# First MLP, first half: three pairs by seven half-size products instead of two, their input's block sums formed a stage earlier and carried through DRAM

## The chip, the cores and the metric

The kernel runs on one core of a Trainium2 chip. The metric is device microseconds of one execution. Before the change the median of three runs is 1082.24 us (1081.54 to 1082.41).

## The reference

A two-layer decoder trunk on a sequence of 512 tokens with 1024 channels. Layer 0 mixes tokens by a short gated convolution, layer 1 by native sparse attention; each layer ends in a squared-ReLU MLP with 4096 hidden channels:

```python
def short_conv_mixer(h, w_in, conv_w, w_out):
    b_gate, c_gate, u = jnp.split(h @ w_in, 3, axis=-1)
    ...
    return (b_gate * conv) @ w_out

def squared_relu_mlp(h, w1, w2):
    return jnp.square(jax.nn.relu(h @ w1)) @ w2

def reference(x, ...):
    for layer in range(DEPTH):
        h = rms_norm(x, norm_mix[layer])
        if layer < N_A_LAYERS:
            x = x + short_conv_mixer(h, a_w_in[layer], a_conv_w[layer], a_w_out[layer])
        else:
            x = x + nsa_mixer(h, b_w_qg[i], b_w_o[i], shared, rel_bias)
        x = x + squared_relu_mlp(rms_norm(x, norm_mlp[layer]), mlp_w1[layer], mlp_w2[layer])
        ...
    return rms_norm(x, final_norm)
```

The change touches layer 0's `w_out` product and the `h @ w1` of layer 0's MLP.

## The kernel before

**Arithmetic.** Inputs and results are 32 bits wide. For TensorE (PE) every matrix is split into a high and a low 16-bit half (`whi`, `wlo` for weights; `xsh`, `xsl` for activations; `rh`, `rl` for the hidden layer), and each product is three matmuls: high by high, high by low, low by high. So every block of weights that arrives in `wst` is converted: ScalarE (ACT) writes the high half (lines 219 and 239), VectorE (DVE) the low half (lines 220 and 240).

**Tiles.** Activations lie with channels on the 128 partitions and the 512 tokens along the row; `X` is the residual stream, eight such chunks. A product is made for one *pair* at a time, 256 output channels, as two PSUM banks of 128 channels by 512 tokens: `pair` runs over eight chunks of input, 48 matmuls of 512 columns (lines 410 to 412). The MLP is done in two halves of 2048 hidden channels: eight pairs of up-projection (`mlp_up`), then four pairs of down-projection (`mlp_down`), and so again. The first half of layer 0's MLP follows directly on the output projection of the convolution mixer (the loop at lines 627 to 637, four calls of `pair`).

**Seven products.** Some pairs are computed by a recursion of Strassen's kind (`seven`, line 672). Weights and activations are seen as two-by-two blocks (128 channels by 128 channels; 128 channels by 256 tokens), and the four block results come from seven block products instead of eight. A seven runs over four double chunks: 84 matmuls of 256 columns (line 687). It needs

- sums of weight blocks: the weights come into `wst2` as blocks, `block_sums` (lines 153 to 158) adds four more blocks on DVE, and seven blocks instead of four are converted (lines 219, 220);
- sums of activation blocks: `form_sums` (line 462) makes, for each of four double chunks, a scaled copy of `X` on ACT (line 465), three DVE operations of `turned_sums` (lines 168 and 170), and a split into halves (lines 431 and 433). They stay in four places (`places`): the tiles `up_s`, and then `ssacc`, `sq` and two of `rb`, which the mean square uses first;
- copies on ACT of the PSUM banks between products (`keep`, line 698) and DVE additions (lines 713, 716, 720) before the squared ReLU.

`UP_SEVEN` says which pairs (0 to 7) of which half are done so; `mlp_pieces` orders the weights accordingly. In before these are pairs 4 and 6 of the first half.

**Where the sums are formed.** In before `early_sums` forms the four blocks of the first half behind pairs 0 and 1. The first two go to their places; the other two are first put into rows of the hidden layer's tiles `rh` and `rl`, since `ssacc`, `sq` and `rb` still hold the mean square, and `move_sums` brings them over by four transfers on GpSimd's (POOL) queue (line 746).

**Around it.** The mean square's root (`ss.rstd`) is made in pair 1, and its broadcast row `rb` (line 376) late in pair 1; only then can `put_relu` treat pairs 0 and 1 (lines 661 to 670: scale and clip, square, `token_sums` for the down-projection, split). A plain pair's result goes through `put_relu` between products of the seven behind it. `ahead` converts weights ahead of use: two plain pieces, or three blocked ones; blocked weights wait behind the root's last operation (`root_op`).

**Queues.** Weights are loaded on SyncE's (SP) queue. Every engine runs its own instructions in the order in which a list scheduler wrote them down: program order is the priority, and work that the planner expects to be ready may be drawn forward. Tiles of the convolution stage lie in a pool `first`, which is closed behind the output projection; the MLP's pool takes over its memory.

Of the kernel before, what the change touches and what calls it, by code (L numbers as in the profile page):

```python
# [10 lines left out]
F32 = mybir.dt.float32  # L11
F16 = mybir.dt.float16
# [39 lines left out]
def body(ctx, tc, x, rel_bias, norm_mix, norm_mlp, mlp_w1, mlp_w2, a_w_in, a_conv_w, a_w_out,  # L52
         kv_norm, w_kv, cmp_pe_k, cmp_pe_v, phi_k_w1, phi_k_w2, phi_v_w1, phi_v_w2,
         b_w_qg, b_w_o, final_norm, ident_c, onehot_c, out):
    nc = tc.nc
# [6 lines left out]
    dram = ctx.enter_context(pool("dram", space=DRAM))  # L62
# [42 lines left out]
            pieces.append(([v[c + k, :, :, c0:c0 + 256] for k in range(2)], None, scale))  # L105

    BY_SEVEN = ((2, 2), (3, 0), (3, 2))
    UP_SEVEN = (((4, 6), (0, 2, 4, 6)), ((6,), (0, 2, 4, 6)))

    v = a_w_in[0].rearrange("(c p) (s n) -> c p s n", p=128, s=3)  # L110
    for c in range(8):
# [67 lines left out]
    def blocked(i):  # L179
        return pieces[i][1] is None  # L180
# [82 lines left out]
    def ahead():  # L263
        while pos["cv"] < len(pieces) and pos["cv"] < pos["use"] + (AHEAD2[0] if blocked(pos["cv"]) else AHEAD):
            yield from convert_piece()

    def drain(gen):
        for _ in gen:
            pass
# [3 lines left out]
    wk = [first.__enter__()]  # L273
# [30 lines left out]
    xt = [xt4[:, t] for t in range(4)]  # L304
# [155 lines left out]
    sums = []  # L460

    def form_sums(sums, c, gname, z, add_up=token_sums):

        for m in range(2):
            ACT.activation(z[:, 2 * m:2 * m + 2].rearrange("p k n -> p (k n)"), X[:, 2 * c + m], AF.Copy,
                           scale=vec[:, gain[gname] + 2 * c + m:gain[gname] + 2 * c + m + 1])
        add_up(z)
        split_to(sums[c][0], sums[c][1], z[:, 4:8])
# [42 lines left out]
    for p in range(4):  # L511
# [57 lines left out]
        for i, dst in enumerate((pc, pu, pb)):  # L569
# [19 lines left out]
            for m in range(2):  # L589
# [9 lines left out]
                elif dst is pu:  # L599
                    if m == 0:  # L600
                        convs = []
                    v = ftile("cv_v", 2, S + 2)
# [21 lines left out]

    xs = new_split(work, "xs")
    ss = SumSq()
    for p in range(4):
        po = [acc(), acc()]
        pair(ys, po)
        if p < 3:  # L630
            drain(ahead())
        for m in range(2):
            residual_in(po[m], 2 * p + m, 1.0 / (SY * SW))
            ss.add(X[:, 2 * p + m])
        for m in range(2):
            split_gain(xs, 2 * p + m, X[:, 2 * p + m], "mlp0")
        drain(ahead())
    first.__exit__(None, None, None)
    NS2[0], NW2[0], AHEAD2[0] = 3, 4, 3

# [4 lines left out]
    def mlp_up(xs, ss, rh, layer, half, rb, sums):  # L645
        gname = f"mlp{layer}"
# [5 lines left out]
        def new_z():  # L652
            return wk[0].tile([128, 8, 256], F32, name="ml_z", bufs=2)
# [72 lines left out]
        def places():  # L726

            tags = 4 * ((wk[0], "up_s", 4),) + ((work, "ssacc", 1), (work, "sq", 1)) + 2 * ((work, "rb", 3),)
            for i in range(0, 8, 2):
                yield [u.tile([128, 4, 256], F16, name=name, bufs=n) for u, name, n in tags[i:i + 2]]  # L730

        def early_sums(c):

            if c < 2:
                sums.append(next(at))
                form_sums(sums, c, gname, new_z(), turned_sums)
            else:
                staged_sums[c] = [u[:, 4 + c, 0:4] for u in rh]
                form_sums(staged_sums, c, gname, new_z(), turned_sums)

        def move_sums():

            for c in (2, 3):
                sums.append(next(at))
                for u, v in zip(sums[c], staged_sums[c]):
                    nc.gpsimd.dma_start(u, v)

        at, staged_sums = places(), {}
        by_seven = UP_SEVEN[layer][half]
        early = half == 0 and layer == 0 and by_seven  # L750
        behind = range(1, 5) if by_seven else range(4, 8)
# [1 line left out]
        held, post, tag = None, iter(()), ""  # L753
        if half == 0:
            ss.thirds()
        for p in range(8):
            own = half or by_seven and p >= by_seven[0]
            tag = ("c" if tag == "a" else "a") if own else ("bcabcb" if by_seven else "bcabcabc")[p]
            if p in by_seven:
                z = new_z()  # L760
                post = put_relu(p, seven(p, xs, z, post, tag), z)
                continue
            drain(post)
            ph = [bank(tag) for _ in range(2)]
            mid = {1: {1: ss.rstd, 6 if early else 4: root_rows}}.get(p) if half == 0 else None
            pair(xs, ph, mid=mid)
            drain(ahead())
            if early and p < 2:
                for c in (2 * p, 2 * p + 1):
                    early_sums(c)  # L770
            if p == 0 and half == 0:
                held = ph
                continue
            if held:
                drain(put_relu(0, held, new_z()))
                held = None
            post = put_relu(p, ph, new_z())
            if p + 1 not in by_seven:
                drain(post)
            if early and p == 2:  # L780
                move_sums()
            if half == 0 and not early and p in behind:
                sums.append(next(at))
                form_sums(sums, p - behind[0], gname, new_z(), turned_sums)
# [105 lines left out]
    with pool("hidden_a") as hp:  # L890
        wk[0] = hp
        rh = first_half(hp, xs, ss, 0)
# [13 lines left out]
    with pool("attn") as ap:  # L906
# [579 lines left out]
        for i in range(len(items) + 6):  # L1486
# [18 lines left out]
            for part in ("stages", "background") if frees else ("background", "stages"):  # L1505
                if part == "background":
                    while credit > 0.0:
                        u = next(bg, "end")
# [21 lines left out]
    with pool("hidden_b") as hp:  # L1530
        wk[0] = hp
        rh = first_half(hp, xs, ss, 1)
        xsh, xsl = (work.tile([128, 2, D], F32, name=n) for n in ("xsh", "xsl"))
        xt = [(xsh, xsl)[t // 2][:, t % 2] for t in range(4)]
# [163 lines left out]
```

## Time and profile before

| | before |
|---|---|
| median of three runs | 1082.24 us |
| the profiled execution | 1083.04 us |
| its span, first to last instruction | 1080.0 us |
| busy PE / DVE / ACT / POOL | 1067.5 / 958.1 / 621.7 / 75.2 us |
| granted TensorE clock over the span | 0.998 |
| output projection, PE | 132.2 to 173.6 us |
| up-projection, first half of layer 0 | 173.6 to 254.8 us |
| down-projection, first half of layer 0 | 254.8 to 328.2 us |

The profile shows one execution. PE is TensorE's matmuls, PEld its weight loads, DVE VectorE, ACT ScalarE, POOL GpSimd, SP SyncE. Rows of groups read: line, engine, operation, output <- inputs, shapes, count, busy time and mean duration, and idle time of the engine ahead of them with what ended it. Rows of the order of time read: start, duration, engine, line, operation, tiles. Durations of neighbouring operations overlap by some 0.1 us.

### The profile page before, as it was taken

How to read it: one execution, taken by the hardware profiler on the slowest of the kernel's cores; microseconds unless marked ns; L12 is line 12 of the kernel's file. 1: busy time of each engine (PE TensorE's matmuls, PEld its weight loads, DVE VectorE, ACT ScalarE, POOL GpSimd, SP SyncE). 2: the span in 40 equal slices, each digit the busy share in tenths (PEclk: the TensorE clock that was granted, in tenths of full speed). 3: DMA queues.
4: the chain of work that ended last, by engine and by line, in shares of the span. 5: the costliest groups of instructions: out<-in, count | busy, mean ns of one | idle time of the engine just before them, and what ended most of it. 6: DMA issues, size and time to landing. Idle time of an engine off the chain costs nothing.

```text
span 1080.0 us, 21256 instructions
## 1 busy us (share of the span) xinstructions
PE 1067.5 (99%) x8486; PEld 740.5 (69%) x8486; DVE 958.1 (89%) x1688; ACT 621.7 (58%) x974; POOL 75.2 (7%) x113
## 2 busy tenths in 40 slices
PE   9999999999999999999999999999999999999997
PEld 4446644477887758874867677775446788766896
DVE  5898757999998999999478899996999999999996
ACT  5663246565334674548577887874666433566453
POOL 1000000000000000000110104211000000002022
PEclk9999999999999999999999999999999999999999
DMA  8344124333433334312443442201542333333221
GB/s 260 112 147 134 40 81 154 125 99 109 137 101 115 104 113 155 119 44 95 126 139 102 143 138 81 61 21 60 166 127 70 106 111 124 98 101 98 98 99 78
DMA packets 117698, 118.50 MB, mean 110 GB/s; under 512 B 7276, under 2 KB 114496, under 8 KB 117600
## 3 DMA queue, kind: packets, MB, share of 16 engines
q1 hardware_dynamic: 114384, 110.77, 32.6%
q10 hardware_dynamic: 2512, 4.70, 1.3%
q0 software_dynamic: 704, 1.68, 0.5%
q8 instruction: 66, 1.08, 0.4%
q14 instruction: 32, 0.26, 0.1%
HBM read 110.22 MB, written 2.14 MB: 104 GB/s over the span
## 4 chain that ended last, share of the span: by engine, by line
PE 72%; DVE 18%; ACT 3%; issue 3%; DMA 3%; POOL 1%; SPq 0%; ACTq 0%; DVEq 0%; POOLq 0%
PE b L833 6%; PE c L411 5%; PE c L410 5%; PE c L412 4%; PE a L833 4%; PE c L833 4%; PE a L412 4%; PE a L687 4%; PE a L410 4%; PE a L411 4%; DVE wlo L220 4%; PE e L833 3%; PE b L412 3%; PE b L411 3%; PE c L1340 3%
## 5 line engine op out<-in xcount | busy, mean ns | idle before, releaser
L219 ACT ACTIVATE whi<-wst 128x1792 f16<-128x1792 f32 x92 | 153.9, 1692 | 120.9 <-DVE wst L158 72.1
L220 DVE SCALAR_TENSOR_TENSOR wlo<-wst,whi 128x1792 f16<-128x1792 f32 x92 | 185.5, 2022 | 6.5 <-ACT whi L219 6.4
L833 PEld LDWEIGHTS <-whi 128*128 128x128 f16 x1768 | 173.0, 98 | 20.3
L240 DVE SCALAR_TENSOR_TENSOR wlo<-wst,whi 128x1024 f16<-128x1024 f32 (+4 forms) x118 | 129.2, 1101 | 20.6 <-ACT whi L239 20.3
L239 ACT ACTIVATE whi<-wst 128x1024 f16<-128x1024 f32 (+4 forms) x118 | 111.1, 950 | 61.8 <-PE a L411 21.9
L412 PEld LDWEIGHTS <-wlo 128*128 128x128 f16 x800 | 78.1, 98 | 86.5 <-DVE wlo L240 1.0
L410 PEld LDWEIGHTS <-whi 128*128 128x128 f16 x800 | 78.2, 98 | 78.9 <-ACT whi L239 0.6
L411 PEld LDWEIGHTS <-whi 128*128 128x128 f16 x800 | 78.2, 98 | 78.4
L833 PEld LDWEIGHTS <-wlo 128*128 128x128 f16 x884 | 86.5, 98 | 10.9 <-DVE wlo L220 0.2
L669 ACT ACTIVATE rh<-ml_z 128x1792 f16<-128x1792 f32 x32 | 54.1, 1693 | 58.2 <-DVE ml_z L164 58.2
L411 PE MATMUL c<-xsl,whi 128*128 128x512 f16 x224 | 85.0, 379 | 0.0
L412 PE MATMUL c<-xsh,wlo 128*128 128x512 f16 x224 | 85.0, 379 | 0.0
L410 PE MATMUL c<-xsh,whi 128*128 128x512 f16 x224 | 85.0, 379 | 0.0
L1327 ACT ACTIVATE at_p<-at_s,at_m 128x384 f32<-128x384 f32 (+3 forms) x128 | 71.0, 556 | 20.9 <-DVE at_m L1325 20.7
L158 DVE TENSOR_TENSOR wst<-wst 128x256 f32<-128x256 f32 x184 | 78.3, 432 | 2.1
L156 DVE TENSOR_TENSOR wst<-wst 128x512 f32<-128x512 f32 x92 | 63.8, 697 | 15.3 <-DMA wst<-mlp_w_dram 15.1
L833 PE MATMUL b<-rh,whi 128*128 128x256 f16 x256 | 69.2, 273 | 0.0
L833 PE MATMUL b<-rh,wlo 128*128 128x256 f16 x256 | 69.2, 273 | 0.0
L833 PE MATMUL b<-rl,whi 128*128 128x256 f16 x256 | 67.8, 273 | 0.0
L687 PEld LDWEIGHTS <-whi 128*128 128x128 f16 x616 | 60.2, 98 | 7.9
L670 DVE TENSOR_TENSOR rl<-ml_z,rh 128x1792 f16<-128x1792 f32 x32 | 64.7, 2023 | 0.4 <-ACT rh L669 0.4
L1325 DVE CUSTOM_DVE_ANT_0 at_s<-b,T 128x384 f32<-128x384 f32 (+3 forms) x128 | 59.1, 485 | 4.9 <-PE b L1318 4.7
(437 smaller groups left out, 2911.7 us busy)
## 6 DMA issues: line engine op xcount, KB each, us to landing
wst<-mlp_w_dram SPq DMA_DIRECT2D x172, 256.0 KB, 2.9
wst<-mlp_w_dram SPq DMA_DIRECT2D x42, 512.0 KB, 3.7
wst<-a_w_in_dram SPq DMA_DIRECT2D x12, 512.0 KB, 3.5
wst<-w_kv_dram SPq DMA_DIRECT2D x12, 512.0 KB, 3.5
wst<-a_w_out_dram SPq DMA_DIRECT2D x8, 512.0 KB, 3.4
wst<-b_w_qg_dram SPq DMA_DIRECT2D x8, 512.0 KB, 3.6
wst<-b_w_o_dram SPq DMA_DIRECT2D x8, 512.0 KB, 3.6
T<-ext_d ACTq DMA_DIRECT2D x6, 528.0 KB, 3.9
```

The lines of the kernel that those rows point to most:

```text
L158: DVE.tensor_tensor(b[:, :, o], b[:, :, x], b[:, :, y], op=OP.add)
L219: ACT.activation(hi, b[:, :, 1:], AF.Copy, scale=sc)
L220: lows[0] = DVE.scalar_tensor_tensor(lo, b[:, :, 1:], sc, hi, op0=OP.mult, op1=OP.subtract)
L239: ACT.activation(hi[:, s:e], w, AF.Copy, scale=sc)
L240: DVE.scalar_tensor_tensor(lo[:, s:e], w, sc, hi[:, s:e], op0=OP.mult, op1=OP.subtract)
L410: PE.matmul(ps, w[0], xs[0], start=start, stop=False, **k)
L411: PE.matmul(ps, w[0], xs[1], start=False, stop=False, **k)
L412: return PE.matmul(ps, w[1], xs[0], start=False, stop=stop, **k)
L670: DVE.tensor_tensor(rh[1][:, p], z[:, 1:8], rh[0][:, p], op=OP.subtract)
L687: PE.matmul(ps[:, 0:256], l, r, start=first and c == 0 and n == 0, stop=c == 3 and n == 2, skip_group_check=not first)
L833: mm = PE.matmul(acc7[i], wl if n == 1 else wh, xl if n == 2 else xh, stop=c == closes[i] and n == 2, start=c == 0 and n == 0 and not othe ...
L1327: self.weighed = ACT.activation(self.p[:, w], lg[:, w], AF.Exp, bias=mn[:, j:j + 1], scale=-1.0, accum_out=l[:, br * 4 + h:br * 4 + h + 1])
```

## The change

Pairs 3, 5 and 7 of the first half are done in seven products instead of pairs 4 and 6 (counted from 1, as in the change's name: 4, 6 and 8). The block sums of the MLP's input are formed in the output projection, one double chunk behind each of its four pairs, in a tile `told` that lies where the convolution's sums lay. From there each block goes to DRAM (`sums_d`) in two transfers on POOL's queue, and `fetch_sums` reads it back on the same queue: two blocks at the start of the up-projection, two behind pair 1, when their places are free. `early_sums`, `move_sums` and the detour through `rh` and `rl` go.

```diff
--- before.py
+++ after.py
@@ -105,7 +105,7 @@
             pieces.append(([v[c + k, :, :, c0:c0 + 256] for k in range(2)], None, scale))
 
     BY_SEVEN = ((2, 2), (3, 0), (3, 2))
-    UP_SEVEN = (((4, 6), (0, 2, 4, 6)), ((6,), (0, 2, 4, 6)))
+    UP_SEVEN = (((3, 5, 7), (0, 2, 4, 6)), ((6,), (0, 2, 4, 6)))
 
     v = a_w_in[0].rearrange("(c p) (s n) -> c p s n", p=128, s=3)
     for c in range(8):
@@ -624,6 +624,8 @@
 
     xs = new_split(work, "xs")
     ss = SumSq()
+    kept_sums = dram.tile([4, 2, 128, 4, 256], F16, name="sums_d")
+    told = wk[0].tile([128, 2, 4, 4, 256], F16, name="xt")
     for p in range(4):
         po = [acc(), acc()]
         pair(ys, po)
@@ -635,6 +637,10 @@
         for m in range(2):
             split_gain(xs, 2 * p + m, X[:, 2 * p + m], "mlp0")
         drain(ahead())
+        form_sums({p: [told[:, k, p] for k in range(2)]}, p, "mlp0",
+                  wk[0].tile([128, 8, 256], F32, name="xz", bufs=1), turned_sums)
+        for k in range(2):
+            nc.gpsimd.dma_start(kept_sums[p, k], told[:, k, p])
     first.__exit__(None, None, None)
     NS2[0], NW2[0], AHEAD2[0] = 3, 4, 3
 
@@ -729,23 +735,14 @@
             for i in range(0, 8, 2):
                 yield [u.tile([128, 4, 256], F16, name=name, bufs=n) for u, name, n in tags[i:i + 2]]
 
-        def early_sums(c):
-
-            if c < 2:
+        def fetch_sums(n):
+
+            for c in range(len(sums), n):
                 sums.append(next(at))
-                form_sums(sums, c, gname, new_z(), turned_sums)
-            else:
-                staged_sums[c] = [u[:, 4 + c, 0:4] for u in rh]
-                form_sums(staged_sums, c, gname, new_z(), turned_sums)
-
-        def move_sums():
-
-            for c in (2, 3):
-                sums.append(next(at))
-                for u, v in zip(sums[c], staged_sums[c]):
-                    nc.gpsimd.dma_start(u, v)
-
-        at, staged_sums = places(), {}
+                for k in range(2):
+                    nc.gpsimd.dma_start(sums[c][k], kept_sums[c, k])
+
+        at = places()
         by_seven = UP_SEVEN[layer][half]
         early = half == 0 and layer == 0 and by_seven
         behind = range(1, 5) if by_seven else range(4, 8)
@@ -753,6 +750,8 @@
         held, post, tag = None, iter(()), ""
         if half == 0:
             ss.thirds()
+        if early:
+            fetch_sums(2)
         for p in range(8):
             own = half or by_seven and p >= by_seven[0]
             tag = ("c" if tag == "a" else "a") if own else ("bcabcb" if by_seven else "bcabcabc")[p]
@@ -765,9 +764,8 @@
             mid = {1: {1: ss.rstd, 6 if early else 4: root_rows}}.get(p) if half == 0 else None
             pair(xs, ph, mid=mid)
             drain(ahead())
-            if early and p < 2:
-                for c in (2 * p, 2 * p + 1):
-                    early_sums(c)
+            if early and p == 1:
+                fetch_sums(4)
             if p == 0 and half == 0:
                 held = ph
                 continue
@@ -777,8 +775,6 @@
             post = put_relu(p, ph, new_z())
             if p + 1 not in by_seven:
                 drain(post)
-            if early and p == 2:
-                move_sums()
             if half == 0 and not early and p in behind:
                 sums.append(next(at))
                 form_sums(sums, p - behind[0], gname, new_z(), turned_sums)
```

## The prediction

> **What bounds the kernel now.** I read the page first (busy shares, the chain), then the busy time by stage, then TensorE's order of work around the change, then groups of VectorE instructions there.
>
> ```profile
> span 1080.0 us, 21256 instructions
> ...
> PE 1067.5 (99%) x8486; PEld 740.5 (69%) x8486; DVE 958.1 (89%) x1688; ACT 621.7 (58%) x974; POOL 75.2 (7%) x113
> ...
> PE 72%; DVE 18%; ACT 3%; issue 3%; DMA 3%; POOL 1%; SPq 0%; ACTq 0%; DVEq 0%; POOLq 0%
> ```
>
> TensorE (PE) has work 99% of the span and is most of the chain of work; VectorE (DVE) is second in both. A shorter PE stage is worth its whole saving as long as DVE keeps up. The next rows cut the time at the points where PE changes stage: output projection, pairs 1 to 3 of the first half's up-projection, pairs 4 to 8, the down-projection, and the second half's up-projection.
>
> ```profile
> 132.16:173.60 41.44, 41.44 (x194) 18.82 (x192) 25.49 (x36) 15.68 (x22) 0.00 (x0) 1.00 0.28 87
> 173.60:205.40 31.80, 31.80 (x161) 14.83 (x160) 30.94 (x50) 23.85 (x28) 2.17 (x4) 1.00 0.54 172
> 205.40:254.84 49.44, 49.44 (x313) 30.54 (x312) 48.31 (x66) 28.06 (x27) 0.00 (x0) 1.00 0.33 105
> 328.20:406.91 78.71, 78.28 (x530) 51.66 (x528) 73.20 (x105) 47.89 (x50) 0.00 (x0) 1.00 0.36 114
> 254.84:328.20 73.36, 73.36 (x673) 65.75 (x672) 69.59 (x104) 30.55 (x22) 0.00 (x0) 1.00 0.33 109
> ```
>
> Columns: stretch and length, busy PE, weight loads, DVE, ACT, POOL, then clock, DMA share, GB/s. PE is busy without a gap in the first three rows, at full clock. DVE is nearly full in both up rows (30.94 of 31.80, 48.31 of 49.44) and has 16 us to spare in the output projection. So the stage is PE's, with DVE close behind.
>
> **The change, part by part.**
>
> *One more pair as seven products.* Numbering pairs 0 to 7, before has 4 and 6 in seven products, after has 3, 5 and 7. The rows are pairs 4, 5, 6 and 7:
>
> ```profile
> 215.78:224.95 9.17, 9.17 (x85) 8.21 (x84) 9.03 (x18) 6.39 (x9) 0.00 (x0) 1.00 0.32 103
> 224.95:235.31 10.36, 10.36 (x50) 4.70 (x48) 9.46 (x12) 4.92 (x4) 0.00 (x0) 1.00 0.49 152
> 235.31:244.48 9.17, 9.17 (x85) 8.21 (x84) 9.08 (x15) 6.94 (x10) 0.00 (x0) 1.00 0.19 57
> 244.48:254.84 10.36, 10.36 (x50) 4.70 (x48) 10.36 (x10) 5.36 (x4) 0.00 (x0) 1.00 0.47 153
> ```
>
> A seven is 84 weight loads with matmuls 256 columns wide in 9.17 us, a plain pair 48 with 512 columns in 10.36. Three sevens in place of two take **1.19 us** off PE. That is all the gain there is on PE. It lies on the path, since PE waits for nothing here.
>
> *What a seven can cost PE.* It copies PSUM out between products (four ACT copies), and PE can wait for them:
>
> ```profile
> L713 DVE TENSOR_TENSOR ml_z<-b,rh x11: 417/420/423, 221.9 to 981.9; 128x256 f32<-128x256 f32 x11
> 395.25 0.27 PE L687 MATMUL a<-up_s,whi 128*128 128x256 f16 x1 [0.43 <-ACT rl L698]
> ```
>
> There are eleven sevens in the kernel (one L713 in each) and one of them waited 0.43 us. One more is worth 0.04 us; I book 0.05, with 0 and 0.43 as ends.
>
> *Work added and moved on DVE and ACT.*
>
> ```profile
> L168 DVE TENSOR_TENSOR ml_z<-ml_z x4: 684/687/693, 178.3 to 189.1; 128x512 f32<-128x512 f32 x4
> L170 DVE SCALAR_TENSOR_TENSOR ml_z<-ml_z x8: 418/423/425, 179.6 to 193.0; 128x256 f32<-128x256 f32 x8
> L433 DVE TENSOR_TENSOR up_s<-ml_z,up_s x2: 1218/1220/1222, 182.6 to 186.3; 128x1024 f16<-128x1024 f32 x2
> L240 DVE SCALAR_TENSOR_TENSOR wlo<-wst,whi x9: 1196/1221/1226, 174.7 to 242.2; 128x1024 f16<-128x1024 f32 x9
> L156 DVE TENSOR_TENSOR wst<-wst x8: 682/691/699, 189.8 to 254.3; 128x512 f32<-128x512 f32 x8
> L158 DVE TENSOR_TENSOR wst<-wst x14: 415/426/433, 193.3 to 240.6; 128x256 f32<-128x256 f32 x14
> L220 DVE SCALAR_TENSOR_TENSOR wlo<-wst,whi x7: 2019/2022/2029, 201.8 to 252.0; 128x1792 f16<-128x1792 f32 x7
> L661 DVE SCALAR_TENSOR_TENSOR ml_z<-ml_z,rb x4: 417/555/691, 224.7 to 248.6; 128x256 f32<-128x256 f32 x2, 128x512 f32<-128x512 f32 x2
> L664 DVE SCALAR_TENSOR_TENSOR ml_z<-c,rb x4: 680/686/689, 197.0 to 238.5; 128x512 f32<-128x512 f32 x4
> L465 ACT ACTIVATE ml_z<-X,vec 128x512 f32<-128x512 f32 x8 | 5.3, 711 | 2.1 <-DVE up_s L433 2.1
> L431 ACT ACTIVATE up_s<-ml_z 128x1024 f16<-128x1024 f32 x2 | 2.1, 1050 | 0.6 <-DVE ml_z L170 0.6
> ```
>
> (DVE rows: min/median/max in ns, first and last start.) One block of sums takes DVE 0.687 + 2 x 0.423 + 1.220 = 2.75 us, and ACT 2 x 0.711 + 1.050 = 2.47. Four blocks leave pairs 0 and 1: 11.0 us of DVE. Three of them go into the output projection: 8.3 us on 25.49 of 41.44, and 7.4 us on ACT's 15.68. Each engine stays under 82% there, behind a PE that waits for nothing; nothing on the path. Without that room (a block between a residual and its gain) the up-projection's inputs would come up to 2.75 us later. The fourth block needs the last residual and stays behind 173.6.
>
> The third seven brings blocked weights: 0.691 + 2 x 0.426 + 2.022 = 3.57 us a piece for a plain 1.22, so 4.7 us for two pieces. Its own DVE steps are three sums (L713, L716, L720, 0.42 each) and three L661 (0.417 + 0.691 + 0.423) for two L664 (1.37): 1.4 more. Together +6.1 us.
>
> *DVE by stretch.* In the stretch of pairs 0 to 2: 30.94 - 11.0 + 2.75, less two plain conversions for pair 3 (2.4), plus the second blocked piece that pair 3 now needs by its start (3.6; the first stands in the place of pair 4's), plus 2.0 for the low half of pair 1's output, which now fell just behind. That is 25.9 of 31.8, so the first seven is fed in time although it starts 10 us earlier. For pairs 3 to 7 the rest of 79.25 - 11.0 + 2.75 + 6.1 = 77.1 remains: 51.2 us in 49.44 - 1.19 = 48.25. **3.0 us of DVE work spill into the down-projection.** The tightest place there is its second pair's first weights:
>
> ```profile
> 266.89 3.96 DVE L220 SCALAR_TENSOR_TENSOR wlo<-wst,whi 128x1792 f16<-128x1792 f32 x2
> ...
> 273.18 0.27 PE L833 MATMUL d<-rh,whi 128*128 128x256 f16 x1
> ```
>
> The first of the two L220 ends at 268.9 and PE wants it at 273.2: 4.3 us of margin, 1.3 after the spill. So I book no stall, with 0 and 2 us as ends. The down-projection then gives DVE 73.36 - 69.59 = 3.8 us back. The second half's up-projection speaks for this: four sevens in turn with pairs, DVE 73.20 of 78.71, and PE lost 0.43 us in all (78.28 busy).
>
> *The detour through DRAM.* Before, four transfers on POOL's queue move two blocks; after, eight writes and eight reads of 256 KB:
>
> ```profile
> L746 POOL DMA_DIRECT2D ssacc<-rh x1 | 0.6, 560 | 182.3 <-ACT rh L431 182.3
> ...
> L746 POOL DMA_DIRECT2D rb<-rl x1 | 0.5, 536 | 1.0 <-DVE rl L433 1.0
> ...
> out_dram<-xsh SPq DMA_DIRECT2D x2, 512.0 KB, 2.8
> ...
> rb<-rl POOLq DMA_DIRECT2D x1, 256.0 KB, 3.0
> ```
>
> An issue holds POOL's queue 0.54 to 0.56 us, a transfer lands in at most 3.0, and a write of 512 KB to DRAM in 2.8. POOL has no other work here (182.3 us idle before its first). Six writes go during the output projection. Before, the last xsl was done about 178; the fourth block takes 2.75 + 1.05, so it is ready about 182. Then come two writes and eight reads, 10 x 0.56: issued by 188, landed by 191. Pair 3 starts at 205.4 and wants sums in its second product, 1.3 us in. 15 us of cover, so it costs nothing; the bounds are 0 and rival C. A transfer through DRAM of 4.2 MB in all in place of 1 is small beside the 87 and 172 GB/s of these rows. The input tile of the sums and the last block's workspace now live until 182 or 185 in memory that the next pool takes over, so the blocked loads on SP's queue (first wanted at the root's end, about 190) and the plain loads behind them may wait some us; the same 15 us cover them.
>
> The Trainium skill, SBUF — State Buffer, section "A bandwidth-pool intuition that's wrong (but worth ruling out)", speaks against this: a transfer issued from GpSimd takes about 0.62 us alone and 3.1 us against a VectorE copy that locks the shared port. The trace's 0.54 to 0.56 us beside a DVE busy 30.94 of 31.80 do not show it; with 3.1 us for each of ten issues an estimate by that page is 182 + 31 + 3 = 216, some 8 us late, and 1089 us.
>
> **The sum.** The profiled execution took 1083.04 us around its span of 1080.0. 1083.04 - 1.19 + 0.05 = 1081.90. The median of the runs, 1082.24, is 0.80 below that execution; on its footing I predict **1081.1**. About 0.2% (2.2 us) is what can be told from no change, so the whole gain, 0.11%, is half of it.
>
> **The rivals.**
>
> A. *DVE is late* by more than the margin of 1.3 us, at the down-projection's second pair or already at pair 3. For it: DVE's two up rows are full, and the last seven now ends at the stage's end, which no stage of before does. Against: the second half's up-projection. Price 0.5 to 2 us: 1081.6 to 1083.1, the gain eaten.
>
> B. *ACT's queue holds a copy back* (the one that ends on the other side, slower). Place: the first copy of pair 3's seven stands in ACT's queue behind a step that waits for DVE, whose work of pairs 0 and 1 can only start when the row scale is there:
>
> ```profile
> 194.43 0.58 ACT L376 ACTIVATE rb<-e 128x512 f32<-128x512 f32 x1
> ACT rh L669 <- DVE ml_z L164: 13.6, 5, 4.7
> ```
>
> The longest such wait of the stage is 4.7 us. PE has one other product to do meanwhile (9.17 / 7 = 1.3), so the price is up to 3.4 us: 1084.5. It makes the kernel slower once the copy is held over 4.6 us; below that it only eats the gain. Against: 6 us of DVE room ahead of pair 3, which should draw these steps forward.
>
> C. *The sums come late.* If each of the ten issues had to wait for one long DVE operation (2.02 us) they would take 2.6 us each: 182 + 26 + 3 = 211, against the 207.7 at which the last block is wanted: 3.1 us, 1084.2; anything above that is slower than before. Against: the four issue rows. The Trainium skill's rule above would be this rival at its dearest, and the chance of C is the chance I give it.
>
> D. *The change does not do what it says*: the additional seven saves nothing net, because PE's margin is returned later in a wait on DVE or DMA. 1082.2.
>
> E. *More than the sum*: the order of the queues is written anew, and gaps elsewhere close. Over 1 us beyond the 1.19 would have to come from the 12.5 us in which PE is not busy. Below 1080.
>
> **How the numbers follow.** My forecast 0.62 (own range 1080.4 to 1081.7: the span of the runs and the copy's 0.43). A 0.15, D 0.04: both within 0.2%. B 0.07 and C 0.05, taken as slower. E 0.07, faster. So faster 0.07, same 0.62 + 0.15 + 0.04 = 0.81, slower 0.12. The range leaves out E and most of B and C: 1079.9 to 1083.6.
>
> **What would show it.** Right: three stretches of 9.17 us in this up-projection, pairs 3, 5, 7; PE without a gap from 173.6 to the down-projection, which starts about 1.2 us earlier; DVE with idle time around 183 to 193 and late conversions afterwards; POOL issues of about 0.55 us, the last landing before 195. Wrong: a PE wait on ACT's L698 copy in pair 3 (B), on wlo about the down-projection's second pair (A), on a transfer from sums_d (C); or PE gaps in other stages.

## The result, and the profile after

| | before | after |
|---|---|---|
| median | 1081.89 us (1081.45 to 1082.41) | 1094.19 us (1092.42 to 1094.96) |
| span of the profiled execution | 1080.0 us | 1092.0 us |

Four runs each. The ratio is 1.0113, 95% interval 1.0101 to 1.0126: the kernel is 12 us slower, where 1.2 us less had been forecast.

The page after, the lines that answer to those of before:

```profile
span 1092.0 us, 21372 instructions
...
PE 1069.8 (98%) x8522; PEld 745.3 (68%) x8522; DVE 964.2 (88%) x1698; ACT 623.5 (57%) x978; POOL 81.7 (7%) x125
...
PE 71%; DVE 18%; issue 4%; DMA 3%; ACT 3%; POOL 1%; SPq 0%; ACTq 0%; DVEq 0%; POOLq 0%
```

PE's busy time rose by 2.3 us, the span by 12.0, so about 10 us are new idle time. The busy time by stage shows where: output projection; pairs 0 to 2; then pairs 3 to 7, one row each (columns as before).

```profile
132.52:173.96 41.44, 41.44 (x194) 18.80 (x192) 33.30 (x48) 22.25 (x31) 3.28 (x6) 1.00 0.35 108
173.96:206.28 32.32, 31.98 (x162) 14.82 (x161) 18.90 (x32) 12.46 (x15) 5.32 (x10) 1.00 0.61 210
206.28:222.56 16.28, 11.17 (x85) 8.96 (x84) 16.28 (x25) 10.62 (x12) 0.00 (x0) 0.90 0.21 64
222.56:232.92 10.36, 10.36 (x51) 4.70 (x48) 10.36 (x14) 4.34 (x3) 0.00 (x0) 1.00 0.48 153
232.92:244.14 11.22, 9.32 (x85) 8.21 (x84) 8.32 (x14) 7.20 (x9) 0.00 (x0) 1.00 0.16 49
244.14:254.50 10.36, 10.36 (x50) 4.70 (x48) 10.36 (x12) 6.16 (x5) 0.00 (x0) 1.00 0.47 153
254.50:265.23 10.73, 9.33 (x86) 8.21 (x84) 10.73 (x18) 5.43 (x7) 0.00 (x0) 1.00 0.34 113
```

The output projection is 41.44 us as before, with DVE at 33.30 instead of 25.49: three block sums fit there for nothing. But the three sevens take 16.28, 11.22 and 10.73 us instead of 9.17, and DVE, nearly full before, is busy 18.90 of 32.32 us ahead of them. PE's idle time there is these five waits (order of time on PE; brackets: idle time and what ended it):

```profile
206.28 0.27 PE L693 MATMUL c<-xsh,whi 128*128 128x256 f16 x1 [0.34 <-DVE ml_z L670]
...
209.43 0.28 PE L693 MATMUL c<-xsh,wlo 128*128 128x256 f16 x1 [2.23 <-DVE wlo L220]
...
214.34 0.27 PE L693 MATMUL c<-up_s,whi 128*128 128x256 f16 x1 [2.88 <-ACT rh L704]
...
242.84 0.27 PE L693 MATMUL c<-up_s,whi 128*128 128x256 f16 x1 [1.90 <-ACT rl L704]
...
258.68 0.27 PE L693 MATMUL c<-up_s,whi 128*128 128x256 f16 x1 [1.40 <-ACT dn_p L704]
```

The account from 173.96 to 265.23, 91.27 us against 81.24: 80.05 were forecast (81.24 - 1.19), the waits add 8.74, and PE is busy 82.53, that is 2.5 longer, mostly in the first seven, whose granted clock is 0.90. With 0.36 us from the start of the kernel the down-projection begins 10.4 us late. Another 1.36 us are lost in the second half's last seven (11.01 us instead of 9.65; taken up with the last experiments). Together 11.75 of the 12.0 us.

**Why DVE stood.** The queues of POOL and SP after, in order of time (x n: issues grouped in one row):

```profile
183.90 0.54 POOL L643 DMA_DIRECT2D sums_d<-xt  x1 [0.72 <-DVE xt L433]
189.13 2.13 POOL L743 DMA_DIRECT2D up_s<-sums_d  x4 [4.69 <-issue]
...
192.30 1.06 POOL L743 DMA_DIRECT2D rb<-sums_d  x2
```

```profile
188.13 2.93 SPq L192 DMA_DIRECT2D wst<-mlp_w_dram  x6
```

Before, the first blocked loads went out here:

```profile
173.84 1.39 SPq L192 DMA_DIRECT2D wst<-mlp_w_dram  x3
```

The last write of sums is issued at 183.90 and lands at 187.99 us; the first blocked weights of the MLP are asked for 0.14 us behind that, 14.3 us later than before. The reads follow 1.0 us later, so six loads and eight reads of 256 KB each, 3.7 MB, run at once. The stretch from 193 to 198, after:

```profile
193.00:198.00 5.00, 5.00 (x24) 2.25 (x23) 0.19 (x1) 1.70 (x1) 0.37 (x1) 1.00 1.03 379
```

The DMA engines are full (share 1.03, 379 GB/s), and the six loads of 256 KB take 2.65, 2.90, 7.15, 8.87, 11.09 and 11.19 us to land. DVE meanwhile:

```profile
191.57 0.69 DVE L156 TENSOR_TENSOR wst<-wst 128x512 f32<-128x512 f32 x1 [4.21 <-DMA wst<-mlp_w_dram]
192.30 0.89 DVE L158 TENSOR_TENSOR wst<-wst 128x256 f32<-128x256 f32 x2
198.53 0.69 DVE L156 TENSOR_TENSOR wst<-wst 128x512 f32<-128x512 f32 x1 [5.34 <-DMA wst<-mlp_w_dram]
199.25 0.89 DVE L158 TENSOR_TENSOR wst<-wst 128x256 f32<-128x256 f32 x2
201.80 0.69 DVE L156 TENSOR_TENSOR wst<-wst 128x512 f32<-128x512 f32 x1 [1.66 <-DMA wst<-mlp_w_dram]
202.41 2.02 DVE L220 SCALAR_TENSOR_TENSOR wlo<-wst,whi 128x1792 f16<-128x1792 f32 x1
204.35 1.28 DVE L670 SCALAR_TENSOR_TENSOR ml_z<-b,rb 128x512 f32<-128x512 f32 x2
```

DVE stands three times, 11.2 us in all, at the sums of weight blocks. Its queue is in order: the scaling of pair 0 (L670) stands behind them and starts at 204.35. Before, the same step started here:

```profile
195.76 1.29 DVE L664 SCALAR_TENSOR_TENSOR ml_z<-b,rb 128x512 f32<-128x512 f32 x2
```

The row scale that it multiplies by is late as well, since ACT's queue stands on the same sums of blocks: `rb` is made at 201.78 instead of 194.43, behind the conversion of the second piece.

```profile
200.18 1.70 ACT L219 ACTIVATE whi<-wst 128x1792 f16<-128x1792 f32 x1 [5.13 <-DVE wst L158]
201.78 0.58 ACT L376 ACTIVATE rb<-e 128x512 f32<-128x512 f32 x1
```

ACT's squares and splits of pairs 0 and 1 wait for the scaling, and the copies of the seven's PSUM stand behind those in ACT's queue:

```profile
210.74 3.28 ACT L675 ACTIVATE rh<-ml_z 128x1792 f16<-128x1792 f32 x2 [2.83 <-DVE ml_z L164]
213.93 0.36 ACT L704 ACTIVATE rh<-c 128x256 f32<-128x256 f32 x1
```

PE's wait of 2.88 us at 214.34 ends with that copy. This is the theory; its rivals are the extra DMA traffic by itself, the third seven with its DVE work, and the order of DVE's queue.

### The profile page after: what moved, and what is told of

Its sections match the earlier page's. It is cut to its first block, busy times and chain, and to the rows that moved or that the text cites. A ratio compares the mean times of both kernels' runs of the same rounds, so it can differ in the third digit from the quotient of the medians.

```text
span 1092.0 us, 21372 instructions
## 1 busy us (share of the span) xinstructions
PE 1069.8 (98%) x8522; PEld 745.3 (68%) x8522; DVE 964.2 (88%) x1698; ACT 623.5 (57%) x978; POOL 81.7 (7%) x125
## 4 chain that ended last, share of the span: by engine, by line
PE 71%; DVE 18%; issue 4%; DMA 3%; ACT 3%; POOL 1%; SPq 0%; ACTq 0%; DVEq 0%; POOLq 0%
PE b L829 6%; DVE wlo L220 5%; PE c L410 4%; PE c L411 4%; PE c L412 4%; PE a L829 4%; PE c L829 4%; PE a L693 4%; PE a L410 4%; PE a L412 4%; PE a L411 4%; PE e L829 3%; PE c L1336 3%; PE d L829 3%; DMA wst<-mlp_w_dram 3%
## 5 line engine op out<-in xcount | busy, mean ns | idle before, releaser
L219 ACT ACTIVATE whi<-wst 128x1792 f16<-128x1792 f32 x94 | 157.2, 1692 | 130.2 <-DVE wst L158 79.0
L220 DVE SCALAR_TENSOR_TENSOR wlo<-wst,whi 128x1792 f16<-128x1792 f32 x94 | 189.0, 2017 | 6.7 <-ACT whi L219 6.6
L240 DVE SCALAR_TENSOR_TENSOR wlo<-wst,whi 128x1024 f16<-128x1024 f32 (+4 forms) x116 | 126.6, 1098 | 17.4 <-ACT whi L239 17.1
L239 ACT ACTIVATE whi<-wst 128x1024 f16<-128x1024 f32 (+4 forms) x116 | 108.9, 948 | 56.8 <-PE a L411 21.0
L412 PE MATMUL c<-xsh,wlo 128*128 128x512 f16 x192 | 72.8, 379 | 0.0
L411 PE MATMUL c<-xsl,whi 128*128 128x512 f16 x192 | 72.8, 379 | 0.0
L410 PE MATMUL c<-xsh,whi 128*128 128x512 f16 x192 | 72.8, 379 | 0.0
```

The source lines that it names most:

```text
L219: ACT.activation(hi, b[:, :, 1:], AF.Copy, scale=sc)
L220: lows[0] = DVE.scalar_tensor_tensor(lo, b[:, :, 1:], sc, hi, op0=OP.mult, op1=OP.subtract)
L239: ACT.activation(hi[:, s:e], w, AF.Copy, scale=sc)
L240: DVE.scalar_tensor_tensor(lo[:, s:e], w, sc, hi[:, s:e], op0=OP.mult, op1=OP.subtract)
L410: PE.matmul(ps, w[0], xs[0], start=start, stop=False, **k)
L411: PE.matmul(ps, w[0], xs[1], start=False, stop=False, **k)
```

## The experiments

Twelve kernels; the median of "before" is 1081.9 to 1082.3 us beside each group. "Opening" below is the issue of the first blocked load on SP's queue.

### Undoing one part: the fourth block, the third seven, the carrying

**Only the fourth block at home.** Blocks 0 to 2 by DRAM; block 3 formed behind pair 0 in the MLP's own memory.

```diff
-        form_sums({p: ...}, p, "mlp0", ...)
-        for k in range(2):
-            nc.gpsimd.dma_start(kept_sums[p, k], told[:, k, p])
+        if p < 3:
+            form_sums({p: ...}, p, "mlp0", ...)
+            for k in range(2):
+                nc.gpsimd.dma_start(kept_sums[p, k], told[:, k, p])
...
+            if early and p == 0:
+                sums[3] = next(at)
+                form_sums(sums, 3, gname, new_z(), turned_sums)
```

> Three sevens as in the change, but only the blocks of output pairs 0 to 2 go through DRAM; the fourth is formed in the up-projection behind pair 0, straight into its place. So the last transfer that reads the old pool's memory is issued near 172.6 us and lands near 177 instead of 188. Theory 'closing' (the blocked weights' loads wait until the old pool is free of its last write, and all else follows from that): loads start near 177, VectorE waits under 3 us in all for weights ahead of pair 3, the three sevens take 9.2 to 9.8 us each, 1080.5 to 1082.5 us. Rival 'capacity' (a third seven, and one that starts 10 us earlier, is more than VectorE and the PSUM copies on ScalarE can feed): loads are early and yet the sevens take 11 to 16 us, 1086 to 1091 us.

Measured: 1082.95 us, ratio 1.0006 (0.9996 to 1.0015). The opening is at 176.49, 0.27 us behind the last landing (176.22), and the three sevens:

```profile
205.41:214.58 9.17, 9.17 (x85) 8.23 (x84) 7.25 (x14) 6.38 (x9) 0.00 (x0) 1.00 0.20 60
...
224.94:234.11 9.17, 9.17 (x85) 8.23 (x84) 8.92 (x14) 6.92 (x10) 0.00 (x0) 1.00 0.20 59
...
244.47:253.76 9.29, 9.29 (x85) 8.21 (x84) 9.29 (x16) 5.43 (x7) 0.00 (x0) 1.00 0.29 96
```

The down-projection starts at 253.76, 1.08 us earlier than before: the forecast gain is there, with the third seven, six reads of sums and the moved DVE work all in place. So none of these costs much by itself; the fourth block's route does. The 1.08 us are lost again later (below), so the time lies half a microsecond above the forecast.

**Carrying alone**, sevens for pairs 4 and 6 as before: `UP_SEVEN = (((4, 6), ...` in the changed kernel.

> The sums are formed in the output projection and carried through DRAM as in the change, but pairs 4 and 6 are the sevens as before. Theory 'closing': loads of blocked weights still start near 188, VectorE still stands about 10 us waiting for them with the squared ReLU of pairs 0 and 1 behind; the first seven comes 10 us later, so only a part reaches TensorE: 1083 to 1088 us. Rival 'capacity': without the third seven nothing is lost, 1081 to 1082.5 us.

Measured: 1086.35 us, ratio 1.0041 (1.0028 to 1.0054). Opening 187.10, DVE stands 8.8 us, the down-projection starts at 258.2, 3.4 us late. The carrying is dear even with two sevens; with three, the first starts 10 us earlier and it is dearer.

**The third seven alone**: `UP_SEVEN = (((3, 5, 7), ...` in the kernel before.

> The kernel before with pairs 3, 5 and 7 as sevens and nothing else changed: sums formed behind pairs 0 and 1, two blocks moved by four transfers. Theory 'closing': loads start near 174, no long wait for weights; VectorE has some 2 us more than it can do ahead of pair 3 (34.1 in 31.8 us), so 1081 to 1084 us. Rival 'capacity': with all four blocks still in the up-projection it is as slow as the change or slower, 1090 us or more.

Measured: 1085.48 us, ratio 1.0032 (1.0021 to 1.0042). Opening 174.14 as before; PE waits 0.5 us for `wlo`, 0.4 and 1.3 for copies, and the down-projection starts at 256.54. The time lies between the two forecasts: the third seven alone loses, but far less than the change. With four block sums left in the up-projection it does not pay; with one of them there, as above, it does.

### Taking pieces of the route away

**No reads.** The reads are replaced by `POOL.memset(sums[c][k], 0.0)`, so the sums' values are left out.

> The change without the eight reads from DRAM; GpSimd writes zeros into the four places instead, so the values of the sums are left out. The writes, and so the late end of the old pool, stay. If the late start (188 instead of 174 us) is the whole loss: 1093 to 1095 us as the change. If the eight reads that run beside the six weight loads make up the greater part (second and third weight piece landing at 198.4 and 201.8): pieces land near 192.5 and 196, VectorE's wait for weights falls from 11.2 to about 5 us, 1084 to 1089 us. Rival 'capacity': no change, 1092 to 1095 us, with little waiting for weights.

Measured: 1087.85 us, ratio 1.0054 (1.0039 to 1.0069). Opening 187.44; the six loads have landed by 195.99 instead of 201.78; DVE stands 6.1 us instead of 11.2. Of the 12.3 us, 6.4 go with the reads and 5.9 stay with the late opening.

**Two blocks at home**: as the first experiment, with `p < 2`.

> Three sevens; only the blocks of output pairs 0 and 1 go through DRAM (four writes, four reads), and the last two are formed in the up-projection behind pair 0, straight into the first two places. The old pool's last transfer lands near 166, so it closes with the last matmul on y as before. Theory 'closing': loads start near 174, no wait of VectorE for weights above 2 us, three sevens of 9.2 to 9.5 us, down-projection near 253.7, 1080.5 to 1082.5 us, no worse than with three blocks carried. Rival (VectorE has no room for one more block ahead of pair 3, 28.6 us of 31.8): PE waits at pair 3 or 5, 1083 to 1086 us.

Measured: 1083.48 us, ratio 1.0016 (1.0007 to 1.0025). Opening 174.19, down-projection at 254.00. The three sevens and the whole up-projection:

```profile
205.77:214.94 9.17, 9.17 (x86) 8.21 (x85) 8.45 (x14) 6.39 (x9) 0.00 (x0) 1.00 0.21 61
225.30:234.47 9.17, 9.17 (x86) 8.21 (x85) 9.17 (x15) 6.92 (x10) 0.00 (x0) 1.00 0.20 58
244.83:254.00 9.17, 9.17 (x86) 8.21 (x85) 9.17 (x16) 5.50 (x8) 0.00 (x0) 1.00 0.32 104
173.95:254.00 80.05, 80.05 (x510) 48.91 (x509) 77.44 (x114) 48.20 (x53) 2.15 (x4) 1.00 0.42 132
```

The stage takes 80.05 us instead of 81.24, the forecast 1.19 less, and PE waits nowhere in it. The time lies in the rival's range, but not for the rival's reason: the stage begins 0.35 us late, the second half's last seven loses 1.33 us (below), and some 0.7 us are lost near 467 and 616 us, which was not followed.

**The fourth block formed, but not written.** Its place is read from block 0 once more, so block 3's values are left out; traffic by reads is the same.

```diff
-        for k in range(2):
-            nc.gpsimd.dma_start(kept_sums[p, k], told[:, k, p])
+        if p < 3:
+            for k in range(2):
+                nc.gpsimd.dma_start(kept_sums[p, k], told[:, k, p])
...
-                    nc.gpsimd.dma_start(sums[c][k], kept_sums[c, k])
+                    nc.gpsimd.dma_start(sums[c][k], kept_sums[c % 3, k])
```

> The change, but the fourth block, formed at the same time in the same tile of the old pool, is not written to DRAM; its place is filled by reading the first block a second time, so the values of the fourth block are left out. Eight reads stay, six writes. If the pool's end waits for the write's landing (188.0) and not for the forming alone (183.6): loads start near 184, 4 us earlier than in the change, and the time falls by 3 to 6 us, 1088 to 1091. If forming the fourth block there is the whole of it, the time stays at 1093 to 1095. If the landing is all of it, 1081 to 1083.

Measured: 1089.51 us, ratio 1.0067 (1.0053 to 1.0081). Opening 183.29 although the last write landed at 175.99: the old memory is held by the forming of block 3 too, not by transfers alone. Each beside its own before, the change is 12.3 us slower and this kernel 7.2: 4.8 us of opening, with two writes fewer, are worth about 5 us.

**The order of DVE's queue.** In the changed kernel three blocked pieces are queued behind the relu of pairs 0 and 1.

```diff
+    relu_op = []
...
-            with tc.issue_after((lows[0] if i == len(pieces) - 1 else root_op[0]).ins):
+            with tc.issue_after((lows[0] if i == len(pieces) - 1 else relu_op.pop() if relu_op else root_op[0]).ins):
...
+            if early and p == 1:
+                relu_op.extend([low] * 3)
```

> The change with one order altered: the block sums of pair 3's second weight piece and of pair 5's two stand on VectorE's queue behind the squared ReLU of pairs 0 and 1 instead of ahead of it. Loads and reads as in the change. Theory 'closing' with the queue's order as its second link (VectorE stands 7 us waiting for the second and third piece while finished pairs 0 and 1 wait behind): the row scale is there near 195, the squared ReLU is done near 205, the second piece near 209, so pair 3 still waits some 3 us for it but the PSUM copies of pairs 3, 5 and 7 run free: 1085 to 1089 us. If the order is of no matter: 1092 to 1095.

Measured: 1090.44 us, ratio 1.0074 (1.006 to 1.0088). Opening unchanged (188.05). The time lies above the theory's range and below the rival's. `rb` is made at 195.31, the scaling of pair 0 starts at 197.38 instead of 204.35, and the sevens take 15.62, 9.17 and 9.71 us: PE's waits in pairs 5 and 7 fall from 3.3 to 0.4 us, but now the first seven waits 4.2 us for its second piece's `whi`. The queue's order was the way by which the delay got from DVE to the later copies; the delay itself comes with the loads.

### The wait for the old memory by itself

The kernel before, untouched but for transfers that nobody reads, out of a tile of the memory that is given over; no third seven, no reads of sums.

```diff
+    spare_d = dram.tile([2, 128, 4, 256], F16, name="sums_d")
+    told = wk[0].tile([128, 2, 4, 256], F16, name="xt")
...
+        if p == 3:
+            DVE.tensor_copy(told[:, 0, 0, 0:128], X[:, 7, 0:128])
+            for k in range(2):
+                nc.gpsimd.dma_start(spare_d[k], told[:, k % 2])
+                if k < 1:
+                    nc.gpsimd.dma_start(told[:, (k + 1) % 2], spare_d[k])
```

This is the version with three transfers in a row; another has two plain writes, another five in a row.

> The kernel before, untouched in its up-projection (products in half size for pairs 4 and 6 alone, block sums formed in the up-projection, no reads), plus two 256 KB transfers by POOL from a tile of the memory that is given over to the MLP to a DRAM tile that nobody reads, issued behind a small copy at the end of the output projection. Theory (the next memory's first loads wait for the landing of the last transfer out of the old one): the transfers land at about 187 to 188 us, SP's blocked loads, at 173.84 us before, are issued within 0.3 us behind that landing, DVE's queue stands 5 to 9 us on the first block sums of weights, and the down-projection starts 2 to 6 us late; time 1084 to 1088 us. Rival (what counts is the reads, the third half-size product or the DVE work added ahead, and not the wait for the memory): loads issued late but covered, or not late at all; within 1 us of before.

> As in the kernel before with one write (products in half size for pairs 4 and 6 alone, no sums carried), there the last write landed at 179.15 us, the blocked loads went out 0.13 us behind it, 5.4 us later than before, and the down-projection started only 0.3 us later, all of it from the start of the kernel. Here the 256 KB go out of the old memory, back into it and out again, one behind the other, so that the last landing should come at about 186 to 188 us, where the changed kernel has it (187.99), with no engine work added. Theory (the wait for the memory is the cause of most of the 12 us): blocked loads at 186 to 188 us, within 0.3 us of the landing; DVE stands on block sums of weights for 5 to 9 us as in the change with two products (8.8), the down-projection starts 1 to 4 us late, time 1083.5 to 1086.5. Rival (the wait for the memory by itself is covered up to 188 us, and the reads or the third product make it dear): loads as late, time within 1.2 us of before.

> The same with five transfers in a row, last landing at about 192 to 196 us, blocked loads right behind. Theory: past the point where the cover ends each microsecond costs about one: down-projection 4 to 8 us later than with three transfers, if these are past that point already, time 1088 to 1094. Rival (the wait for the memory is not what costs): within 1.5 us of before.

| transfers | last landing | opening | down-projection later than before, less the shift of the kernel's start | time, ratio |
|---|---|---|---|---|
| two side by side | 179.15 | 179.28 | 0.0 | 1083.32, 1.0011 (1.0003 to 1.002) |
| three in a row | 186.84 | 187.02 | 4.7 | 1087.78, 1.0043 (1.0029 to 1.0058) |
| five in a row | 192.99 | 193.32 | 8.8 | 1090.80, 1.0081 (1.0068 to 1.0094) |

(The shift, +0.3, +0.6 and -0.2 us, is read at the end of the output projection.) The first forecast missed: the copy was ready at 175.4, not at 184, and an opening at 179.3 is still covered. Its opening 0.13 us behind the landing is what it shows. The other two show that the wait costs: an opening at 187, a microsecond ahead of the changed kernel's, costs the kernel before 4.7 us with only the transfers added, more than the 1 to 4 forecast. The rows of the version with three in a row, DVE, ACT, SP and POOL:

```profile
182.23 0.55 POOL L645 DMA_DIRECT2D sums_d<-xt  x1 [2.88 <-DMA xt<-sums_d]
```

```profile
186.99 2.56 ACT L465 ACTIVATE ml_z<-X,vec 128x512 f32<-128x512 f32 x4 [6.56 <-DMA sums_d<-xt]
```

```profile
187.02 2.93 SPq L192 DMA_DIRECT2D wst<-mlp_w_dram  x6
```

```profile
188.35 0.69 DVE L168 TENSOR_TENSOR ml_z<-ml_z 128x512 f32<-128x512 f32 x1 [6.66 <-ACT ml_z L465]
```

The write lands at 186.84, and both ACT's first write into the new memory and SP's first load start 0.15 to 0.18 us behind it: two different tiles held by one transfer. I had expected DVE to stand on the loads; here it stands 6.66 us on ACT's `ml_z`, because block sums are formed there in this kernel. The cause is the same, the first user another, and so the 4.7 us are not the price in the changed kernel. For that the runs above stand: 5.9 us with no reads, and about 5 us for 4.8 us of opening.

### The second half's last seven

In the changed kernel and in the first experiment this seven loses 1.36 and 1.28 us more than before. The DVE row that it hangs on, before and with the fourth block at home:

```profile
388.11 0.69 DVE L156 TENSOR_TENSOR wst<-wst 128x512 f32<-128x512 f32 x1 [1.18 <-DMA wst<-mlp_w_dram]
```

```profile
388.31 0.69 DVE L156 TENSOR_TENSOR wst<-wst 128x512 f32<-128x512 f32 x1 [2.43 <-DMA wst<-mlp_w_dram]
```

The load takes 3.19 us before and 4.44 there. In the DMA table over just these loads one line is new:

```profile
q8 instruction: 1, 0.02, 1.2%
```

It is one of 67 packets of 16 KB that carry instructions; they come once in about 256 of PE's 17044 instructions, take 0.9 to 2.2 us each over the kernels, and lie elsewhere in each. The Trainium skill, Runtime: NRT & Kernel Launch, section "Instruction fetch mechanics", has the same blocks of 256 instructions in 16 KB and calls their cost mostly hidden; here PE shows no wait for the block itself, but a load in flight is delayed. Two kernels move them, by more and shorter products on zeros at the start (30 and 84 PE instructions more):

```diff
-    keep_busy(7)
+    keep_busy(22, 128)      # fourth block at home
+    keep_busy(49, 64)       # kernel before
```

> This is the kernel with only blocks 0 to 2 by DRAM, whose up-projection gains 1.08 us and whose fourth half-size product of half 1 gives it back. In its trace a 16 KB packet of the queue that carries instructions (67 packets in the run, one for every 256 or so of TensorE's 17044 instructions) starts at 385.68 us, in the middle of the weight loads issued at 383.37 and 383.78 us, and the second of them lands after 4.44 us; before, the packet starts at 390.82 us, the load lands after 3.19 us. The edit: TensorE's seven 512-column products on zeros at the start become 22 of 128 columns, that is 30 TensorE instructions more ahead of everything, so that each 16 KB packet should come 30 instructions earlier in the program. Theory (the packet delays the load, DVE stands on the load, TensorE on DVE): the packet starts at about 382.5 us, the load lands after about 3.2 us, the fourth product takes 9.1 to 9.7 us instead of 10.93, half 1's down-projection starts 1.2 to 1.8 us earlier, the time falls to about 1081.4 us (1080.7 to 1082.2) unless another packet falls on another load that is waited for. Rival (the late landing belongs to the kernel's order of loads and to DVE, not to the code): the load still takes 4.4 us and the product 10.9, time 1083 as without the edit.

> The kernel before with TensorE's seven 512-column products on zeros at the start as 49 of 64 columns, 84 TensorE instructions more ahead of everything. The counterpart of the run with the code moved by 30: here the 16 KB packet of instructions that starts at 390.82 us before should come 84 instructions earlier, at about 386 us, among the weight loads issued at 384.42 and 384.83 us. Theory (code on a load that is waited for): the second load lands after 4.2 to 4.9 us instead of 3.19, the fourth half-size product of half 1 takes 10.7 to 11 us instead of 9.65, and half 1's down-projection starts about 1.2 us later than before, besides what the start itself costs (up to 1 us, to be read at the first real product). Rival: the load lands after 3.2 us wherever the packet is, and the product stays at 9.65.

| | packet | load issued, landed | seven starts, takes |
|---|---|---|---|
| before | 390.82, after the load | 384.83, 388.02 (3.19) | 386.79, 9.65 |
| after | 397.08, within | 395.13, 399.76 (4.63) | 397.18, 11.01 |
| fourth block at home | 385.68, within | 383.78, 388.22 (4.44) | 385.71, 10.93 |
| the same, code moved | 384.48, ahead | 386.76, 389.98 (3.21) | 388.30, 10.10 |
| before, code moved | 388.45, within | 387.97, 392.09 (4.12) | 390.57, 9.94 |

The packet delays the load, both ways: moved off, 3.21; moved on, 4.12. In the fourteen kernels this load took 4.12 to 4.88 us in the seven where a packet starts in the midst of it, 2.95 to 3.21 in the six where none does, and 3.17 in one where it starts 0.4 us ahead of the landing. And the seven (counted here from its first matmul's start to its last one's, 0.11 us less than in the rows by stage) takes 9.06 us plus what the load lands later than 0.64 us after its start: 0.59, 1.94, 1.87, 1.04, 0.88 by that, 0.59, 1.95, 1.87, 1.04, 0.88 measured; the same sum holds within 0.02 us in all fourteen kernels, down to 0 where the load lands earlier. But the forecasts of length missed, since the loads were also issued earlier or later against the seven (0.6 us earlier with the code moved in before, 0.4 later in the other), and the times are no better: 1085.70 us, ratio 1.0034 (1.0022 to 1.0046), and 1087.26 us, 1.005 (1.0038 to 1.0063). The short products delay the first product on weights (7.13 us instead of 6.63, and 7.50 instead of 6.10), and the output projection ends 1.6 and 3.8 us late, which is more than that. Where the rest comes from, and what sets when the loads are issued, was not followed. No version beat the kernel before.

## Why the prediction was wrong

Right: the size of the gain on PE (1.19 us; 1.08 seen with one block at home, 1.19 with two), the output projection's room for three block sums, three stretches of 9.17 us where DVE is in time, a down-projection in which PE did not wait, and POOL's issues (0.54 to 0.58 us after; the Trainium skill's 3.1 us, SBUF — State Buffer, section "A bandwidth-pool intuition that's wrong (but worth ruling out)", is not seen beside these VectorE operations, nor the rival that rested on it). The transfers landed some 10 us later than forecast, but that PE wait on a transfer of `sums_d` which was named for it did not come: the last read landed at 201.28.

The step that failed is *the detour through DRAM*, and in it the sentence that blocked loads "may wait some us; the same 15 us cover them". Three things in it were wrong:

1. *When the memory opens.* I had 182 or 185, the end of the tiles' use by engines. A write's own landing belongs to it, 4.1 us after its issue at 183.90, and the first blocked load stands behind it: 188.13. I also took 2.8 us for a write, from a row on another queue at the end of the kernel; on POOL's queue here the eight took 4.5 us in the median.
2. *Whose cover it is.* The 15 us ran to PE's first use at 205.4. The first user is DVE, which has to make two pieces ready (2 x 3.57) and, in the same queue, relu and splits of pairs 0 and 1 (scaling 2 x 1.28, token sums 2 x 1.54, low halves 3.96, by their rows): 16.7 us. By this estimate, from the first landings at 191 that ends at 208 with no wait at all. The cover was gone, and 2 us more, before any transfer met another. The 25.9 of 31.8 us that I called "fed in time" is a sum over a stretch; it held no order, and DVE could not use the time ahead of the loads.
3. *Traffic.* Means of 87 and 172 GB/s say nothing of a burst. Reads and loads set free by the same event came together, 379 GB/s, and a load that takes 2.65 us took 11.19. By the run without reads this is 6.4 of the 12.3 us.

Rivals A and B both happened, at pair 3: PE waited 2.23 us for `wlo` and 2.88 for the copy that B named. But B was priced from the longest wait of an undisturbed trace (up to 1084.5), and each was thought of as an accident of its own; they were two ends of one late load. The 0.43 us as the upper end for what one seven costs PE was too low as well: copies alone took 6.2 us in the three. (Rival C's own terms give 3.3 us where 3.1 stands; nothing hangs on it.)

The parts are not additive, since one wait covers another: the opening costs 4.7 us in the kernel before, the eight reads 6.4 us if the opening is late, and six or four of them nothing measurable in the stage when it is early. That the whole memory opens at once, and not tile by tile where addresses overlap, rests on two tiles seen to start together and on block 3's forming holding the loads with no write; a layout with the carried tile in memory that nobody takes over wasn't tried.

## What to carry to other kernels

Before adding a transfer out of memory that is about to be handed over, take its landing, not its issue, as the moment of handover, and ask which engine's queue uses the new memory first and how much of its in-order work lies between that and the bottleneck; the cover ends there, not where the bottleneck looks. Count what else is released at the same moment, because transfers that start together share one limit. Moving all but the last piece of a job can bring the whole gain in the stage; look for where it is lost next.

## What the runs showed that I had not expected

- PE's clock can fall after a wait. In the first seven after, behind waits of 2.23 and 2.88 us, the granted clock was 0.50 for 3.4 us, and matmuls of 256 columns came 0.21 us apart instead of 0.11:

```profile
215.35:218.76 3.41, 3.41 (x19) 2.41 (x17) 3.41 (x6) 1.55 (x4) 0.00 (x0) 0.50 0.00 0
```

```profile
216.14 0.42 PE L693 MATMUL b<-xsh,wlo 128*128 128x256 f16 x1
216.36 0.42 PE L693 MATMUL b<-xsl,whi 128*128 128x256 f16 x1
...
219.39 0.27 PE L693 MATMUL c<-ssacc,wlo 128*128 128x256 f16 x1
219.50 0.27 PE L693 MATMUL c<-sq,whi 128*128 128x256 f16 x1
```

  The seven was busy 11.17 us instead of 9.17: beside 5.1 us of waits it lost 2.0 more. The Trainium skill, TensorE: Matmul & The Clock Gate, section "HAM oscillation — how this bites in real kernels", asks for no idle gap over about 3.4 us; here the longest gap was 2.88. In the kernel whose fourth block is not written, a gap of 3.41 us that ends at 211.51 left the clock at 1.00:

```profile
211.50:215.00 3.50, 3.49 (x32) 3.13 (x32) 3.50 (x5) 1.57 (x3) 0.00 (x0) 1.00 0.00 0
```

  So the length of one gap did not decide. That short gaps add up is not shown either: with the carrying alone, gaps of 1.67 and 1.97 us close together left it at 1.00. What decided stays open.
- Where a kernel's code is fetched matters to a load: one 16 KB packet in the midst of a 256 KB load went with 4.1 to 4.9 us instead of 3.0 to 3.2, so PE instructions added or dropped far ahead can add or take about a microsecond at a load that is waited for.
- Landing times of one size on one path: 256 KB from memory on the chip to DRAM by POOL's queue 3.8 to 5.1 us in the kernels that carry sums, 2.3 to 4.7 in those with added transfers alone; 256 KB of weights around the handover 2.5 to 12.4 us.
